# Moving only the later half of the queries in the recurrence heads of a hybrid decoder layer

## The chip, the cores and the metric

The kernel runs on one core of a Trainium2 chip. The metric is the time of one execution in device microseconds. Engines are named as in the profile: PE (TensorE; PEld is its loading of stationary operands), DVE (VectorE), ACT (ScalarE), POOL (GpSimd) and SP, whose queue issues most transfers.

## The reference

One layer over 1040 tokens (16 meta tokens and 1024 real ones), model width 1024:

```
h = h + 1/2 * SwiGLU_1(RMSNorm(h))
u = RMSNorm(h) @ W_in
o = concat[ HGRN2(u_hgrn) , StickBreaking(u_sb) ]
h = h + o @ W_out
h = h + 1/2 * SwiGLU_2(RMSNorm(h))
```

The change lies in HGRN2, a gated linear recurrence with four heads of key and value width 128, worked in chunks of 128 tokens:

```
bcum = cumsum(log f);  decay[t,s] = exp(bcum[t] - bcum[s]) for s <= t
attn[t,s] = sum_d q[t,d] k[s,d] decay[t,s,d];   o = (q exp(bcum)) S + attn v
S_new = exp(b_last) S + (k exp(b_last - bcum))^T v
```

followed by a normalisation of each head's output and a gate. The decay differs for each key column d, so the attention inside a chunk is no single matmul.

## The kernel before, in words

All projections and both feed-forward parts are matmuls in halves: an operand is split into a rounded high part (`wh`, `xh`, `oT`...) and a low part, and three products are summed. The recurrence works in plain float32, and each of its 128x128 matmuls shows in the trace as two passes (two LDWEIGHTS, two MATMUL).

`hgrn_attend(h, ...)` is a generator that does one recurrence head. It builds the attention of all eight chunks by levels n = 1, 2, 4, 8, 16, 32, 64. At level n a chunk is cut into blocks of 2n tokens, and the later n tokens of each block attend to the earlier n. The tiles hold the factors up to the block borders: QA is the query side, KB the key side (head dimension on partitions, tokens along the row), and F and `Ts` hold products of forget factors. A level has three parts.

- Scores (`scores`, L855): for each chunk KB is the stationary operand and QA the moving one, all 128 queries of it. Four chunks fill one PSUM bank, tile `lvl` of pool `pz`; a level fills two such banks, and the pool has two.
- Only the part where later queries meet earlier keys is kept in `attn`: by a predicated copy on DVE up to n = 8 (L886), by block copies on ACT from n = 16 on (L877).
- Then DVE multiplies QA and KB by their factors (L904, L908) and makes the next `Ts` (L914). These overwrite what the scores read, and the next level's scores need them.

After the levels the head transposes KB (`km` for the meta tokens, `knp`, L920 and L927), copies them to SBUF, makes the state of the first chunk from the meta tokens (`s`, L934, copied by DVE at L935) and the updates (`up`, L941), and runs the state through the chunks on DVE (L944). Two halves of the output follow (`op`, L954 and L957), with squares and roots on ACT, a multiplication on DVE (L967), transposes (`onp`, L973), gain and gate (L975) and a split into oH (L980, L981). At its start it transposes the values (`flip`, tile vT) and copies the meta part `vm` on DVE (L845).

PSUM here has four pools of two banks: `pz` (tag z), `ptr` (tag tr), `po` (tag o) and `pproj2`, for the product that runs beside the heads. With a tag's two banks in turn, a tile waits until the last reader of the tile two before it is done.

The heads are woven by `weave` with the first half of the product o @ W_out: 64 steps of three `wo` matmuls (L1267) on the attention heads' output oT. Below, heads 0 to 3 are A to D; A, B and C run beside each other, and D follows A. `weave` writes the order of PE by hand: each `yield a, b` of a head states the PE time a that the step took and the delay b until its next step is due, and two totals (the last arguments) set how the product's steps are spread over the heads' work. So the yielded numbers fix PE's order, which is kept as written. The order on DVE, ACT, POOL and SP is made by a scheduler from estimates. Each engine works its own order strictly in turn.

## Time and profile before

| | |
|---|---|
| median of 3 runs (lowest to highest) | 2064.65 us (2059.46 to 2064.86) |
| the profiled execution | 2062.77 us |
| its span, first to last instruction | 2061.0 us |
| granted TensorE clock | 1.000 |
| busy: PE, DVE, ACT, POOL | 2004.8, 1376.6, 901.2, 638.6 us |
| MATMUL passes of `lvl` (L855) | 512, from 1215.6 to 1340.7 us |

Times inside the execution are microseconds from the start of the span. The four heads with the first half of the product last from about 1213 us to 1369 us; before that come the first feed-forward part, the projections and the attention heads, after it the second half of the product and the second feed-forward part. A busy PE in the page is an upper figure: a matmul's row lasts longer than the step from one matmul to the next, since they are pipelined. What PE really needs is read from the starts of consecutive rows.

### The profile page before, as it was taken

What the parts mean: (1) busy time and instruction counts of PE and PEld (TensorE: products, weight loads), DVE (VectorE), ACT (ScalarE), POOL (GpSimd) and SP (SyncE); (2) the same over time, 40 slices, a digit from 0 to 9 for tenths busy, and PEclk for the clock granted to TensorE, in tenths of its full rate; (3) what the DMA queues carried; (4) which work ended last, traced back from release to release, by engine and by line L of the source; (5) the groups of instructions that cost most, each with busy time, mean ns of one, the idle gap of its engine ahead of it and who ended that gap; (6) DMA issues with size and microseconds to landing.
All of it is one profiled execution on the core that took longest, in us unless ns stands there. A gap on an engine that the chain in (4) does not pass through costs nothing.

```text
span 2061.0 us, 31571 instructions
## 1 busy us (share of the span) xinstructions
PE 2004.8 (97%) x11249; PEld 1782.3 (86%) x11249; DVE 1376.6 (67%) x2069; ACT 901.2 (44%) x1855; POOL 638.6 (31%) x696
## 2 busy tenths in 40 slices
PE   7999999999999999999999999999999999999999
PEld 7999999999987899988887878888888888878887
DVE  6867745556688842257878757648677677666774
ACT  7633332334554534456666623336333333234443
POOL 2366644542000002243443300210564454441000
PEclk9999999999999999999999999999999999999999
DMA  8643322227875645435454262684343333349573
GB/s 237 192 145 113 112 79 94 99 76 232 285 219 171 226 135 169 147 123 130 116 144 114 64 223 88 195 272 137 112 131 105 95 110 102 97 150 346 185 229 113
DMA packets 289647, 314.96 MB, mean 153 GB/s; under 512 B 24080, under 2 KB 218000, under 8 KB 289488
## 3 DMA queue, kind: packets, MB, share of 16 engines
q1 hardware_dynamic: 272304, 260.83, 41.1%
q0 software_dynamic: 16144, 52.10, 6.6%
q8 instruction: 89, 1.46, 0.3%
q14 instruction: 70, 0.57, 0.1%
q10 hardware_dynamic: 1040, 0.00, 0.0%
HBM read 228.62 MB, written 84.23 MB: 152 GB/s over the span
## 4 chain that ended last, share of the span: by engine, by line
PE 83%; DVE 7%; DMA 3%; ACT 3%; issue 2%; POOL 0%; SPq 0%; DVEq 0%; POOLq 0%; ACTq 0%
PE o L599 16%; PE qb L313 15%; PE qa L313 10%; PE qc L313 10%; PE proj L162 5%; PE proj L160 5%; PE proj L161 5%; PE qd L313 4%; PE o L561 3%; PE wo L1267 3%; PE flip L1086 2%; DVE wl L270 1%; PE lvl L855 1%; DVE keep L1232 1%; PE oacc L1156 1%
## 5 line engine op out<-in xcount | busy, mean ns | idle before, releaser
L313 PE MATMUL qb<-T,wh 128*128 128x384 f32 (+1 forms) x1056 | 317.8, 362 | 0.0
L270 DVE TENSOR_TENSOR wl<-s,wh 128x512 fp32r<-128x512 f32 x176 | 198.8, 1130 | 95.2 <-ACT wh L268 91.1
L313 PEld LDWEIGHTS qb<-T,wh 128*128 128x128 f32 x1056 | 195.8, 188 | 21.5
L313 PE MATMUL qa<-B,wh 128*128 128x384 f32 (+1 forms) x704 | 213.9, 367 | 0.3 <-ACT sg L415 0.3
L599 PE MATMUL o<-wl,th 128*128 128x512 f32 x539 | 209.9, 391 | 3.7 <-DVE wl L520 3.7
L599 PE MATMUL o<-wh,tl 128*128 128x512 f32 x539 | 209.6, 390 | 0.7 <-DVE tl L520 0.7
L599 PE MATMUL o<-wh,th 128*128 128x512 f32 x539 | 209.9, 391 | 0.0
L268 ACT CAST wh<-s 128x512 fp32r<-128x512 f32 x176 | 109.4, 621 | 223.2 <-PE qb L313 164.1
L160 PE MATMUL proj<-xh,wh 128*128 128x384 f32 (+2 forms) x576 | 205.0, 356 | 0.2 <-ACT xh L250 0.2
L270 DVE TENSOR_TENSOR wl<-raw,wh 128x512 fp32r<-128x512 f32 x184 | 170.1, 926 | 52.2 <-ACT wh L268 48.7
L161 PE MATMUL proj<-xh,wl 128*128 128x384 f32 (+2 forms) x576 | 199.1, 346 | 0.0
L162 PE MATMUL proj<-xl,wh 128*128 128x384 f32 (+2 forms) x576 | 198.9, 345 | 0.1
L268 ACT CAST wh<-raw 128x512 fp32r<-128x512 f32 x184 | 113.6, 620 | 184.1 <-PE qc L313 100.4
L313 PE MATMUL qb<-T,wl 128*128 128x384 f32 (+1 forms) x528 | 192.0, 364 | 0.9 <-DVE wl L270 0.9
L518 ACT CAST th<-act 128x512 fp32r<-128x512 f32 (+2 forms) x176 | 96.6, 550 | 178.1 <-PE o L599 120.0
L520 DVE TENSOR_TENSOR tl<-act,th 128x512 fp32r<-128x512 f32 (+2 forms) x176 | 105.5, 602 | 64.9 <-ACT th L518 63.7
L313 PE MATMUL qd<-X,wh 128*128 128x272 f32 x704 | 144.4, 292 | 2.0 <-DVE sp L397 1.6
L283 POOL TENSOR_TENSOR s<-raw 128x512 f32<-128x512 f32 x88 | 122.6, 1393 | 74.8 <-DVE wl L270 60.1
L313 PEld LDWEIGHTS qa<-B,wh 128*128 128x128 f32 x704 | 130.5, 188 | 16.5 <-ACT sg L415 0.7
L1232 DVE TENSOR_TENSOR_SCAN keep<-keep 128x144 f32<-128x144 f32 (+6 forms) x112 | 127.1, 1138 | 8.3 <-ACT keep L1228 6.0
L1237 POOL TENSOR_TENSOR sig<-sig,keep 128x144 f32<-128x144 f32 (+3 forms) x64 | 88.2, 1378 | 141.7 <-DVE keep L1232 75.6
L313 PE MATMUL qa<-B,wl 128*128 128x384 f32 (+1 forms) x352 | 128.8, 366 | 0.8 <-DVE wl L270 0.8
(343 smaller groups left out, 4761.1 us busy)
## 6 DMA issues: line engine op xcount, KB each, us to landing
raw<-in_ffn_w_in_dram SPq DMA_DIRECT2D x228, 256.0 KB, 3.0
raw<-in_ffn_w_out_dram SPq DMA_DIRECT2D x176, 256.0 KB, 4.3
raw<-in_w_in_dram SPq DMA_DIRECT2D x28, 512.0 KB, 4.5
ks<-kD SPq DMA_DIRECT2D x32, 260.0 KB, 5.6
oT<-oD SPq DMA_DIRECT2D x32, 256.0 KB, 4.7
ak<-in_ffn_w_out_dram SPq DMA_DIRECT2D x22, 256.0 KB, 5.3
v<-vD SPq DMA_DIRECT2D x8, 576.0 KB, 4.8
vD<-vhl SPq DMA_DIRECT2D x8, 512.0 KB, 3.9
```

What stands on the lines that cost most here:

```text
L160: nc.tensor.matmul(ps, wh[:, s], xs, start=k == 0, stop=False)
L161: nc.tensor.matmul(ps, wl[:, s], xs, start=False, stop=False)
L162: nc.tensor.matmul(ps, wh[:, s], xl[:, k, c0 : c0 + n], start=False, stop=k == nk - 1)
L268: nc.scalar.copy(hi, src)
L270: nc.vector.tensor_sub(lo, src, hi.bitcast(F32))
L283: op(t, x, y)
L313: nc.tensor.matmul(ps, a[:, k, :], b[:, k0 + k, :], start=start and k == 0 and i == 0, stop=k == 3 and i == 2, skip_group_check=True,)
L518: nc.scalar.copy(hi, src)
L520: nc.vector.tensor_sub(lo, src, hi.bitcast(F32))
L599: nc.tensor.matmul(banks[bank][m], z[:, m * P : (m + 1) * P], y, start=start and q == 0 and e == 0, stop=q == nq - 1 and e == 2, skip_grou ...
L1232: nc.vector.tensor_tensor_scan(out=kv, data0=kv, data1=kv, initial=1.0 if last else keep[:, end : end + 1], op0=ALU.mult, op1=ALU.bypass,)
L1237: nc.gpsimd.tensor_mul(sig, sig, keep[:, 1 : nk + 1])
```

## The change

It has five edits, all in `hgrn_attend` and the call of `weave`.

1. From n = 4 on, the scores move only the later-half queries of each block: a matmul has 64 moving columns where it had 128, and the eight chunks of a level fill one bank where they filled two. The stationary operand and the number of matmuls stay. The copies become one of 512 elements per partition in place of two of 256 (n = 4, 8), and half as many on ACT, twice as wide.
2. A level's factors on QA and KB are written ahead of its copies into `attn`.
3. The small tiles `vmp`, `km` and `s` go from the tr banks to the o banks.
4. The copies of `vm` and of the first state go from DVE to ACT.
5. Levels from n = 4 yield 960 in place of 1740, and the total work handed to `weave` is 4 * 18000 in place of 4 * 21900.

```diff
-        ps = self.flip(vT, [(0, META)])
-        nc.vector.tensor_copy(vm, ps[:META, 0, :])
+        ps = self.po.tile([P, P], F32, tag="o", name="vmp")
+        nc.tensor.transpose(ps[:META, :], vT[:, :META], self.ident)
+        nc.scalar.copy(vm, ps[:META, :])
...
         def later(x, n):
 
+            if len(x.shape) == 3:
+                return x.rearrange("p c (b h r) -> p c b h r", h=2, r=n)[:, :, :, 1, :]
             return x.rearrange("p (b h r) -> p b h r", h=2, r=n)[:, :, 1, :]
 
         def level(i, n):
+
             nb = P // (2 * n)
-            m = later(self.masks[:, i, :], n).unsqueeze(1).broadcast_to([P, 4, nb, n])
-            for half in range(2):
-                ps = scores(half)
-                if n >= 16:
-                    for s in range(0, P, 2 * n):
-                        nc.scalar.copy(
-                            attn[half][s : s + n, :, s + n : s + 2 * n],
-                            ps[s : s + n, :, s + n : s + 2 * n],
-                        )
-                    continue
-                out, src = (
-                    x.rearrange("p c (b h r) -> p c b h r", h=2, r=n)[:, :, :, 1, :]
-                    for x in (attn[half], ps)
+            m = later(self.masks[:, i, :], n)
+            if n < 4:
+                m = m.unsqueeze(1).broadcast_to([P, 4, nb, n])
+                return [
+                    (later(attn[half], n), m, later(scores(half), n)) for half in range(2)
+                ]
+            ps = self.pz.tile([P, 8, P // 2], F32, tag="z", name="lvl")
+            for c in range(8):
+                nc.tensor.matmul(
+                    ps[:, c, :].rearrange("p (b r) -> p b r", r=n),
+                    KB[:, META + c * P : META + (c + 1) * P],
+                    later(QA[:, c * P : (c + 1) * P], n), start=True, stop=True,
                 )
-                nc.vector.copy_predicated(out, m, src)
+            if n < 16:
+                m = m.unsqueeze(1).broadcast_to([P, 8, nb, n])
+                return [(later(at8, n), m, ps.rearrange("p c (b r) -> p c b r", r=n))]
+            return [
+                (at8[s : s + n, :, s + n : s + 2 * n], None, ps[s : s + n, :, s // 2 : s // 2 + n])
+                for s in range(0, P, 2 * n)
+            ]
...
         for i, n in enumerate(LEVELS):
-            level(i, n)
+            copies = level(i, n)
...
                 kb[:, :, 0, :], kb[:, :, 0, :], tk[:, :, 1:2].broadcast_to([P, nb, n])
             )
+            for out, m, got in copies:
+                if m is None:
+                    nc.scalar.copy(out, got)
+                else:
+                    nc.vector.copy_predicated(out, m, got)
...
-            yield 1740, 2600
+            yield 960 if n >= 4 else 1740, 2600
         dec = tn
 
-        km = self.ptr.tile([P, P], F32, tag="tr", name="km")
+        km = self.po.tile([P, P], F32, tag="o", name="km")
...
-        ps = self.ptr.tile([P, P], F32, tag="tr", name="s0")
+        ps = self.po.tile([P, P], F32, tag="o", name="s0")
         nc.tensor.matmul(ps, kms, vm, start=True, stop=True)
-        nc.vector.tensor_copy(S[:, 0, :], ps)
+        nc.scalar.copy(S[:, 0, :], ps)
...
-                        self.weave(first_half_of_o(), lanes, 64 * 680.0 + 5000.0, 4 * 21900.0)
+                        self.weave(first_half_of_o(), lanes, 64 * 680.0 + 5000.0, 4 * 18000.0)
```

The edits also move instructions. On PE, in the levels of heads A, B and C, before (one row per run of like matmuls; `lvl` are scores, `wo` the product beside):

```order
L1086 MATMUL flip<-ident,vT 128x128 x8
L855 MATMUL lvl<-QA,KB 128x128 x168
L920 MATMUL km<-ident,KB 16x128
L927 MATMUL knp<-ident,KB 128x128 x8
L920 MATMUL km<-ident,KB 16x128
L927 MATMUL knp<-ident,KB 128x128 x8
```

The same stretch now, up to the second group of `wo`:

```order
L1100 MATMUL flip<-ident,vT 128x128 x8
L856 MATMUL lvl<-QA,KB 128x128 x48
L884 MATMUL lvl<-QA,KB 128x64 x16
L1281 MATMUL wo<-wh,oT 128x512
L1281 MATMUL wo<-wl,oT 128x512
L1281 MATMUL wo<-wh,oT 128x512
L856 MATMUL lvl<-QA,KB 128x128 x8
L884 MATMUL lvl<-QA,KB 128x64 x16
L1281 MATMUL wo<-wh,oT 128x512
L1281 MATMUL wo<-wl,oT 128x512
L1281 MATMUL wo<-wh,oT 128x512
L884 MATMUL lvl<-QA,KB 128x64 x24
```

Three more such groups of three follow, so that 15 `wo` matmuls stand ahead of the first `km` where none did. From there on the count of `wo` that stand ahead of each step is 15 higher than before, up to the last `op` of head D.

On DVE, at level n = 2 of heads A and B, before (`wl` is the low part of a W_out tile, split for `wo`; the L886 rows are the copies into `attn`):

```order
L886 COPY_PREDICATED attn<-masks,lvl 128x128x2 x2
L904 TENSOR_TENSOR QA<-QA,Ts 128x256x2
L908 TENSOR_TENSOR KB<-KB,Ts 128x260x2
L886 COPY_PREDICATED attn<-masks,lvl 128x128x2
L914 TENSOR_TENSOR Ts<-F 128x520
L886 COPY_PREDICATED attn<-masks,lvl 128x128x2
L904 TENSOR_TENSOR QA<-QA,Ts 128x256x2
L908 TENSOR_TENSOR KB<-KB,Ts 128x260x2
```

And now:

```order
L913 TENSOR_TENSOR QA<-QA,Ts 128x256x2
L917 TENSOR_TENSOR KB<-KB,Ts 128x260x2
L924 COPY_PREDICATED attn<-masks,lvl 128x128x2 x2
L147 TENSOR_TENSOR wl<-raw,wh 128x512 x2
L924 COPY_PREDICATED attn<-masks,lvl 128x128x2
L928 TENSOR_TENSOR Ts<-Ts 128x130
L913 TENSOR_TENSOR QA<-QA,Ts 128x256x2
L917 TENSOR_TENSOR KB<-KB,Ts 128x260x2
L924 COPY_PREDICATED attn<-masks,lvl 128x128x2
```

The factors stand ahead of the copies, and two splits stand inside level n = 2: of these the first stood behind level n = 8 of A and B, the second behind the first factors of n = 16. The third to fifth splits now stand ahead of A's and B's level n = 8.

On PE, at the end of head D, before (the last `op` of its second half, then the product, then the transposes of its output, then the product again, ending on oH, the heads' own output):

```order
L957 MATMUL op<-vr,attn 128x128
L1267 MATMUL wo<-wh,oT 128x512
L1267 MATMUL wo<-wl,oT 128x512
L1267 MATMUL wo<-wh,oT 128x512 x2
L1267 MATMUL wo<-wl,oT 128x512
L1267 MATMUL wo<-wh,oT 128x512 x2
L1267 MATMUL wo<-wl,oT 128x512
L1267 MATMUL wo<-wh,oT 128x512 x2
L1267 MATMUL wo<-wl,oT 128x512
L1267 MATMUL wo<-wh,oT 128x512 x2
L1267 MATMUL wo<-wl,oT 128x512
L1267 MATMUL wo<-wh,oT 128x512
```

Then come the eight `onp` rows and nine more `wo` on oT. Now:

```order
L971 MATMUL op<-vr,attn 128x128
L1281 MATMUL wo<-wh,oT 128x512
L1281 MATMUL wo<-wl,oT 128x512
L1281 MATMUL wo<-wh,oT 128x512 x2
L1281 MATMUL wo<-wl,oT 128x512
L1281 MATMUL wo<-wh,oT 128x512 x2
L1281 MATMUL wo<-wl,oT 128x512
L1281 MATMUL wo<-wh,oT 128x512
L987 MATMUL onp<-ident,vT 128x128 x8
L1281 MATMUL wo<-wh,oH_13950 128x512
```

Nine `wo` stand between the last `op` and `onp` in place of 15, and none on oT stand behind `onp`.

On SP's queue the load of the second normalisation's gain (`g2r`) now stands ahead of the first six loads of the second feed-forward part's weights; it stood behind them. On ACT, seven high parts of W_out tiles now stand ahead of the first copy of a level n = 16; two did.

## The prediction

> **What bounds the kernel now.** I read the page first: its busy shares and, in the chain that ended last, the shares by engine.

> ```profile
> PE 2004.8 (97%) x11249; PEld 1782.3 (86%) x11249; DVE 1376.6 (67%) x2069; ACT 901.2 (44%) x1855; POOL 638.6 (31%) x696
> PE 83%; DVE 7%; DMA 3%; ACT 3%; issue 2%; POOL 0%; SPq 0%; DVEq 0%; POOLq 0%; ACTq 0%
> ```

> PE bounds the kernel as a whole, so a change gains where it takes work from PE or lets it idle less. The heads are one stretch of it. The second view is the table by windows over that stretch: start and end, length, then busy time (instructions) of PE, PEld, DVE, ACT and POOL, granted clock, DMA share, GB/s.

> ```profile
> 1215.00:1245.00 30.00, 26.61 (x212) 24.20 (x211) 28.07 (x50) 3.48 (x6) 0.00 (x0) 1.00 0.53 178
> 1245.00:1265.00 20.00, 19.33 (x163) 18.35 (x162) 18.39 (x41) 9.98 (x39) 0.00 (x0) 1.00 0.17 53
> 1265.00:1283.00 18.00, 14.33 (x101) 11.94 (x100) 11.36 (x28) 7.07 (x16) 0.00 (x0) 1.00 0.39 122
> 1305.00:1340.00 35.00, 34.05 (x213) 29.98 (x213) 23.41 (x38) 8.37 (x28) 5.73 (x8) 1.00 0.65 199
> ```

> DVE is nearly always busy while heads A, B and C make their small levels; later PE is nearly full. The real need of PE follows from starts: sixteen score matmuls of head D took 1.79 us as pieces of the chain (0.112 each pass), six of the product 1.40 (0.233 each).

> ```profile
> 1304.99 1.79 PE lvl L855 x16
> 1306.78 1.40 PE wo L1267 x6
> ```

> In the first two windows no product runs: 212 x 0.112 = 23.7 of 30 us and 163 x 0.112 = 18.3 of 20 us. PE idles 6.3 and 1.7 there, 8.0 together. The third view, groups by line and tile over the stretch, says for whom `lvl` waited at the PE itself (4.3 us) and what the copies cost.

> ```profile
> L855 PE MATMUL lvl<-QA,KB 128*128 128x128 f32 x512 | 63.7, 279 | 4.3 <-DVE attn L886 2.5 <-ACT attn L877 1.3 <-DVE attn L864 0.2
> L886 DVE COPY_PREDICATED attn<-masks,lvl 128x256 f32<-128x256 uint8 x32 | 17.7, 577 | 4.4 <-PE lvl L855 4.0
> ```

> **Edit 1, narrow scores.** 4 heads x 5 levels x 8 matmuls x 2 passes = 320 passes move 64 columns in place of 128. No score of before does that. The nearest row is a matmul that moves a single column through a 128x128 stationary operand (L173, elsewhere in the kernel), seen in three short windows of the timeline, each of which begins one pass later:

> ```profile
> 569.99 0.47 PE L173 MATMUL nps<-ones_d,nacc 128*128 128x1 f32 x3
> 570.10 0.47 PE L173 MATMUL nps<-ones_d,nacc 128*128 128x1 f32 x3
> 570.21 0.38 PE L173 MATMUL nps<-ones_d,nacc 128*128 128x1 f32 x3
> ```

> These start 0.11 us apart with one column moved, as against 0.112 with 128. So the pass is set by something that the edit leaves alone, and that comes once per matmul; the load of the stationary operand is the candidate. I take 0: between 1 and 128 columns lie 0.002 us, at most 0.6 us for all 320 passes. The other bound is a pass half as long, 0.056, 17.9 us of PE work; what that would give is a rival below.

> [...]

> The copies on DVE up to n = 8 become one of 512 elements. From DVE's timeline, where x2 means two in a row:

> ```profile
> 1248.19 0.77 DVE L886 COPY_PREDICATED attn<-masks,lvl 128x256 f32<-128x256 uint8 x2
> 1248.87 0.68 DVE L904 TENSOR_TENSOR QA<-QA,Ts 128x512 f32<-128x512 f32 x1
> 1249.47 0.69 DVE L908 TENSOR_TENSOR KB<-KB,Ts 128x520 f32<-128x520 f32 x1
> 1250.38 0.68 DVE L147 TENSOR_TENSOR wl<-raw,wh 128x512 fp32r<-128x512 f32 x1
> ```

> Two copies take 0.68 us from start to next start, one multiplication of 512 elements 0.60. One copy of 512 lies between 0.60 and 0.68: at most 0.08 x 6 = 0.5 us on the busy DVE of A to C.

> **Edits 2 and 5, with one bank per level: the order.** By the new order 15 `wo` stand ahead of the first `km`, one group of three per round of levels from n = 4 on, and five splits (`wl`, 0.61 us each on DVE) move up into n = 2 to n = 8. There DVE is the full engine (28.07 of 30 us), so its part grows by 5 x 0.61 = 3.1, less some of the 0.5 of the copies: +2.7. The two groups of `wo` there (2 x 3 x 0.233 = 1.4) fit into PE's 6.3 idle. Three groups, 2.1 us, fall in the rounds from n = 16, where three heads need 48 x 0.112 = 5.4 us of PE a round against 3 x (0.60 + 0.61) = 3.6 of DVE: there PE pays. Factors ahead of copies, and a level that needs one bank, take away part of the 4.3 us that `lvl` waited, and the splits leave that part of DVE: I give them 0.8. So the levels of A to C end 2.7 + 2.1 - 0.8 = 4.0 later, and everything behind has 15 x 0.233 = 3.5 us less to do: **+0.5**. Bounds: nothing longer (-3.5) and 3.1 + 2.1 longer (+1.7).

> **Edits 3 and 4: small tiles and copies.** The waits view for PE, on the stretch (total, times, longest):

> ```profile
> PE knp L927 <- ACT vT L928: 1.2, 2, 0.7
> PE flip L1086 <- DVE vm L845: 1.1, 1, 1.1
> PE op L954 <- ACT sq L962: 0.8, 1, 0.8
> PE lvl L855 <- ACT attn L877: 0.9, 1, 0.9
> PE km L920 <- DVE F L944: 0.9, 1, 0.9
> PE s L934 <- DVE F L944: 0.7, 1, 0.7
> PE up L941 <- DVE F L935: 0.4, 1, 0.4
> PE knp L927 <- DVE kms L921: 0.4, 1, 0.4
> ```

> Between the levels and head C's transposes `km` and `s` waited for tr banks that DVE's state steps (L944) had to leave; the o banks are free then for A and B, and the state copy leaves DVE. Of 1.2 + 0.9 + 0.7 + 0.4 + 0.4 = 3.6 us, those for `km`, `s`, `up` and `kms` (2.4) should go, with a little of the first: **-2.6**, between -1.2 (only `km` and `s` less what `knp` then waits) and -3.6.

> Against it, `s` of head C stands amid the outputs of A and B. Its o bank is the one that L967 of the first of these must leave. Timelines of PE and DVE:

> ```profile
> 1287.03 0.48 PE L934 MATMUL s<-vm,kms 16*128 16x128 f32 x2
> 1287.44 1.83 PE L941 MATMUL up<-vr,vT 128*128 128x128 f32 x14
> 1289.29 0.68 DVE L967 TENSOR_TENSOR vT<-op,ss 128x512 f32<-128x512 f32 x1
> 1290.12 0.46 PE L954 MATMUL op<-F,QA 128*128 128x128 f32 x2 [0.84 <-ACT sq L962]
> ```

> `s` ran at 1287.03, and the third `op` already waited for a bank, until 1290.12. Now `s` cannot start before 1289.29 + 0.68 = 1289.97; with `s` and `up` (0.41 + 1.7) behind it the third `op` comes at about 1292.1: **+2.0**. Bounds: 0, if the order of bank release leaves another one free, and 1289.97 - 1287.03 = 2.9. Queued behind `s` are `up`, the outputs and, by DVE's state steps, head C.

> The wait of `flip` for `vm` goes, since `vmp` no longer takes a tr bank (**-1.1**; 0 if the copy on ACT is as late). Of the waits of `lvl` for ACT one of 0.9 stands in head D; with one bank per level it goes (**-0.9**; 0 to -0.9).

> **The end of head D.** Nine `wo` (2.1 us) in place of 15 (3.5) now cover the work between the last `op` and `onp`. Before:

> ```profile
> 1363.28 0.69 DVE L967 TENSOR_TENSOR vT<-op,ss 128x512 f32<-128x512 f32 x1
> 1365.71 1.04 PE L973 MATMUL onp<-ident,vT 128*128 128x128 f32 x8
> 1365.91 0.62 ACT L145 CAST wh<-raw 128x512 fp32r<-128x512 f32 x1 [2.88 <-PE wo L1267]
> 1366.35 1.41 DVE L975 SCALAR_TENSOR_TENSOR attn<-onp,og,KB 128x512 f32<-128x512 f32 x2 [1.74 <-PE onp L973]
> ```

> `vT` was done at 1363.97, about 3.0 us after the last `op`, so 2.1 us of cover leave 0.9. ACT now has casts (0.62) between the squares, and half 0's gain (L975, 1.41 / 2) may stand ahead of half 1's multiplication. I take 0.9 + 0.7: **+1.6**, between 0 and 0.9 + 0.62 x 2 + 0.7 + 0.9 = 3.7, the last 0.9 for `onp` itself with nothing beside it.

> **Outside the heads.** The gain `g2r` is now loaded ahead of six weight tiles. Before:

> ```profile
> 1381.15 1.29 DVE L238 SCALAR_TENSOR_TENSOR xn<-hm,rs,g2r 128x1024 f32<-128x1024 f32 x1 [1.69 <-DMA g2r<-in_ffn_norm_dram]
> 1383.09 0.50 PE L1267 MATMUL wo<-wh,oH 128*128 128x512 f32 x1 [0.63 <-DVE hm L1693]
> ```

> DVE stood 1.69 for it, and PE behind DVE 0.63: **-0.8** (0 to -1.1). Two `vm` copies on ACT at the heads' start delay `vr`: **+0.3** (0 to 0.6).

> Sum: 0 + 0.5 - 2.6 + 2.0 - 1.1 - 0.9 + 1.6 - 0.8 + 0.3 = -1.0. The profiled execution took 2062.77 us, so 2061.8; it lies 1.9 below the median of the runs shown, by which it would be 2063.6. I say 2062.5. The low bounds add up to -0.6 - 3.5 - 3.6 - 1.1 - 0.9 - 1.1 = -10.8, the high ones to 1.7 - 1.2 + 2.9 + 3.7 + 0.6 = +7.7; half of each, since they will not fall together, gives the forecast's own range of 2057 to 2067.

> **Rivals.** (1) The narrow pass costs half. Then 80 passes of head D save 80 x 0.056 = 4.5 us where PE is full; of the 240 of A to C, where DVE keeps pace, at most PE's share from n = 16, 144 x 0.056 = 8.1, less what DVE limits, some 6. 2061.8 - 10.5 = 2051. For: half the columns. Against: the one-column rows. By this rival edit 1 does what its words promise, and by the forecast it does not.

> (2) All 15 `wo` fall into PE's 8.0 us of idle ahead of `km`, the levels end no later: 2061.8 - 4.0 = 2057.8. For: 8.0 exceeds 3.5. Against: DVE's 28.07 of 30, to which the splits come.

> (3) Slower: the splits in the full DVE part wait for their weights. The third split needs the third raw tile, whose buffer comes free with the first split; in between lie a load and a cast (0.62), against about 4.7 us of DVE work standing between the two splits. Rows of the loads (median us from issue to landing) and of the chain of waits:

> ```profile
> raw<-in_w_out_dram SPq DMA_DIRECT2D x10, 256.0 KB, 2.8
> 1204.69 8.75 DMA QA<-hg_q
> ```

> At 2.8 it fits. A load as long as the heads' own, 8.75, gives a stall of 8.75 + 0.62 - 4.7 = 4.7 on DVE with the factors of three heads queued behind it, and delayed casts on ACT hold the copies from n = 16 for another 1: 2061.8 + 5.7 = 2067.5, slower than before. It decides from a landing of about 4 us. For: seven casts stand ahead of the first copy of n = 16. Against: few other loads run then.

> **How the numbers follow.** Forecast 0.60, rivals 0.11, 0.17 and 0.12. A measurement here tells about 0.3%, 6.2 us, from no change. Faster than 2058.4 are the first rival, half of the second and 0.06 of the forecast: 0.25. Slower than 2070.9 are a third of the third and 0.05: 0.09. The range goes from 2053 to 2069: the first rival and the ends of the third lie outside.

> **What would show it.** Starts of 64-column passes 0.11 apart (0.056 would make rival 1 right); `wl` rows without a DMA ahead of them between 1225 and 1250; the first `km` about 4 us later; `s` of C waiting for L967; idle PE ahead of D's `onp`; no wait for `g2r`. A first `km` not later at all means that I took DVE for too full, and wrong waits in the outputs that the bank terms fail.

## The result: slower by 0.8%, at a lower TensorE clock

| | median (lowest to highest), us | runs | ratio to before, 95% interval |
|---|---|---|---|
| before | 2064.09 (2059.46 to 2066.57) | 7 | |
| changed | 2082.33 (2067.65 to 2085.47) | 7 | 1.008 (1.0064 to 1.0096) |

I forecast no measurable change, 2062.5 us within 2053 to 2069. The measured time lies 13 us above the range. The profiled execution of the changed kernel took 2079.49 us, its span is 2077.7 us, and its mean granted TensorE clock is 0.990 where it was 1.000.

The page of the changed kernel: busy shares, the granted clock in 40 slices of 51.9 us, and the chain of waits by engine.

```profile
PE 2019.2 (97%) x11249; PEld 1799.4 (87%) x11249; DVE 1374.3 (66%) x2053; ACT 898.1 (43%) x1835; POOL 639.1 (31%) x696
PEclk9999999999999999999999997999999999999999
PE 87%; DVE 7%; ACT 2%; issue 2%; DMA 1%; POOL 0%; SPq 0%; DVEq 0%; POOLq 0%; ACTq 0%
```

PE is busy for 14 us more with the same 11249 matmuls, and one slice of the clock, from 1246.6 us, reads 7 tenths. The table by windows of the changed kernel (columns as before: PE, PEld, DVE, ACT, POOL, granted clock, DMA share, GB/s) shows where. Before, the clock was 1.00 in every such row.

```profile
1213.00:1245.00 32.00, 26.17 (x187) 24.36 (x187) 29.76 (x55) 4.42 (x8) 0.00 (x0) 0.89 0.54 179
1245.00:1265.00 20.00, 17.59 (x113) 16.73 (x112) 12.93 (x23) 4.01 (x12) 0.00 (x0) 0.77 0.11 34
1265.00:1290.00 25.00, 24.82 (x120) 23.78 (x120) 9.38 (x16) 6.55 (x15) 0.57 (x1) 0.57 0.22 66
1290.00:1370.00 80.00, 75.47 (x486) 66.39 (x486) 51.46 (x96) 24.45 (x84) 14.47 (x17) 0.98 0.62 196
```

From 1265 to 1290 us PE is busy nearly all the time, and does 120 matmuls in 25 us; DVE and ACT wait. Pieces of the chain of waits say what a narrow pass costs there:

```profile
1249.40 3.53 PE lvl L884 x32
1257.50 6.73 PE lvl L884 x32
1270.11 10.13 PE lvl L884 x48
1284.93 0.21 PE km L934
```

32 passes take 3.53 us at full clock, 0.110 each, and 6.73 us, 0.210 each, a few microseconds later. In windows of 4 us the clock reads 0.50 from 1257 to 1285 without a break.

First and last starts of scores and `km` place the loss (before, then changed; L856 are the wide scores, n = 1 and 2 and the diagonal):

```profile
L855 PE MATMUL lvl<-QA,KB x512: 270/275/377, 1215.6 to 1340.7; 128*128 128x128 f32 x171
L920 PE MATMUL km<-ident,KB x3: 272/272/277, 1266.4 to 1279.5; 128*16 128x128 f32 x3
```

```profile
L856 PE MATMUL lvl<-QA,KB x192: 271/275/423, 1211.9 to 1335.9; 128*128 128x128 f32 x192
L934 PE MATMUL km<-ident,KB x3: 273/273/421, 1284.7 to 1295.7; 128*16 128x128 f32 x3
```

From the first score to the first `km` it takes 1284.7 - 1211.9 = 72.8 us in place of 50.8. The same reading of the kernels below, from starts in their profiled executions (the stages follow each other; "km C" is the last `km` of heads A to C; the first score comes at 1211.9 us in one execution and at 1218.3 us in another, so these stages compare better than the ends of spans; e11_best_wo, e12_wo3, e13_wo6 and e15_best2 are told in the text only):

| kernel | first score to first km | to km C | to first op | to last op of D | to the end | median time, us | ratio to before, 95% interval | median clock |
|---|---|---|---|---|---|---|---|---|
| before | 50.8 | 13.1 | 3.9 | 77.5 | 700.2 | | | |
| changed | 72.8 | 11.0 | 4.8 | 80.5 | 696.7 | 2082.33 | 1.008 (1.0064 to 1.0096) | 0.990 |
| e1_wide | 62.7 | 10.2 | 4.8 | 79.0 | 696.4 | 2070.66 | 1.004 (1.0026 to 1.0055) | 0.9965 |
| e2_narrow | 63.3 | 17.3 | 4.3 | 76.3 | 701.0 | 2077.81 | 1.0076 (1.0058 to 1.0094) | 0.990 |
| e3_order | 58.4 | 13.3 | 5.4 | 80.5 | 696.5 | 2067.82 | 1.0024 (1.0013 to 1.0035) | 0.997 |
| e4_keys | 61.3 | 9.7 | 4.8 | 77.2 | 696.7 | 2064.06 | 1.0017 (1.0003 to 1.0031) | 0.996 |
| e5_trim | 48.3 | 14.2 | 6.0 | 76.4 | 700.9 | 2062.63 | 0.9995 (0.9986 to 1.0004) | 0.997 |
| e6_first | 61.2 | 12.9 | 3.9 | 77.7 | 699.8 | 2072.83 | 1.0047 (1.0029 to 1.0066) | 0.9985 |
| e7_banks | 50.7 | 10.2 | 4.8 | 80.4 | 700.0 | 2062.80 | 0.9996 (0.9987 to 1.0005) | 0.998 |
| e8_trim_km | 48.1 | 13.7 | 7.5 | 74.2 | 699.6 | 2060.36 | 0.9984 (0.9973 to 0.9994) | 0.997 |
| e9_copies | 72.1 | 12.1 | 7.8 | 78.6 | 699.7 | 2085.49 | 1.0113 (1.0092 to 1.0133) | 0.9865 |
| e10_best | 48.1 | 12.6 | 7.7 | 74.2 | 700.5 | 2060.14 | 0.9977 (0.9964 to 0.9989) | 0.997 |
| e14_moving | 50.4 | 15.0 | 6.3 | 77.1 | 699.9 | 2067.25 | 1.0014 (1.0005 to 1.0023) | 0.997 |

In the rows from e1_wide on the ratio is to runs of before on the same chip, whose medians lie between 2062.9 and 2065.3.

The waits for which PE idled in the changed kernel (total, times, longest):

```profile
PE lvl L856 <- DVE attn L924: 5.2, 6, 2.1
PE s L948 <- ACT sq L976: 2.5, 1, 2.5
PE onp L987 <- DVE vT L981: 2.0, 1, 2.0
PE lvl L884 <- ACT attn L922: 2.0, 2, 1.1
PE lvl L884 <- DVE attn L924: 1.1, 2, 0.6
PE knp L941 <- ACT vT L942: 0.7, 1, 0.7
```

They explain few of the 22 us. Two theories stood against each other at this point. **M**: the clock follows the share of time in which PE moves columns, and a narrow pass, which lasts as long as a wide one (0.110 us at full clock against 0.112), halves it. **S**: the clock falls because of stalls, which the new order on DVE makes longer in n = 1 and 2.

### The profile page after: what moved, and what is told of

Same layout as the page of the kernel before. It is cut to its first block, busy times and chain, and to the rows that moved or that the text cites. A ratio compares the mean times of both kernels' runs of the same rounds, so it can differ in the third digit from the quotient of the medians.

```text
span 2077.7 us, 31530 instructions
## 1 busy us (share of the span) xinstructions
PE 2019.2 (97%) x11249; PEld 1799.4 (87%) x11249; DVE 1374.3 (66%) x2053; ACT 898.1 (43%) x1835; POOL 639.1 (31%) x696
## 4 chain that ended last, share of the span: by engine, by line
PE 87%; DVE 7%; ACT 2%; issue 2%; DMA 1%; POOL 0%; SPq 0%; DVEq 0%; POOLq 0%; ACTq 0%
PE o L599 17%; PE qb L313 15%; PE qa L313 10%; PE qc L313 10%; PE proj L160 5%; PE proj L162 5%; PE proj L161 5%; PE wo L1281 4%; PE qd L313 4%; PE o L561 3%; PE lvl L884 2%; PE flip L1100 2%; DVE wl L270 2%; DVE keep L1246 1%; PE lvl L856 1%
## 6 DMA issues: line engine op xcount, KB each, us to landing
raw<-in_ffn_w_in_dram SPq DMA_DIRECT2D x228, 256.0 KB, 3.1
raw<-in_ffn_w_out_dram SPq DMA_DIRECT2D x176, 256.0 KB, 4.2
oT<-oD SPq DMA_DIRECT2D x32, 256.0 KB, 4.3
ak<-in_ffn_w_out_dram SPq DMA_DIRECT2D x22, 256.0 KB, 5.1
```

## Experiments: what lowers the clock

**e1_wide, wide scores put back.**

```diff
-            ps = self.pz.tile([P, 8, P // 2], F32, tag="z", name="lvl")
-            for c in range(8):
-                nc.tensor.matmul(... later(QA[:, c * P : (c + 1) * P], n) ...)
+            got = [scores(half) for half in range(2)]
```

> The changed kernel, but the scores from n = 4 on again move all 128 queries of a chunk into two banks per level; factors first, the small tiles' banks, the copies on ACT, and the order of PE stay as changed. Theory M (the TensorE clock falls where PE moves too few columns for its time, and narrow passes, 0.112 us apart at full clock with half the columns, do that): granted clock 1.00 from 1240 us on, the mean at 0.998 or more, first km near 1270 instead of 1284.7, time 2057 to 2064. Theory S (the clock falls because PE stalls 1 to 2.4 us at a time in levels n = 1 and 2, where five weight splits came forward on DVE): the stalls are still there, the clock is 0.50 for some 30 us again, time 2075 to 2085.

The table by windows of e1_wide and its waits:

```profile
1237.00:1253.00 16.00, 11.25 (x86) 10.31 (x86) 14.34 (x30) 2.48 (x4) 0.00 (x0) 1.00 0.30 92
1253.00:1285.00 32.00, 29.35 (x229) 26.79 (x229) 19.75 (x39) 12.84 (x48) 0.57 (x1) 1.00 0.22 71
```

```profile
PE lvl L856 <- DVE attn L918: 11.2, 12, 2.1
```

The clock is 1.00 through the levels with the stalls there, longer in sum than as changed (11.2 us against 5.2): as the only cause of the fall S fails, and M holds for the clock. But M's time does not: 2070.66 in place of at most 2064, and the first `km` 62.7 us after the first score. Something besides the clock lengthens the levels by 12 us.

**e2_narrow, narrow scores alone.** The kernel before with edit 1 only (score and copies of the changed kernel, copies where they were).

> The kernel before with only the narrow scores and their one bank and merged copies from n = 4 on; order of PE, place of the copies, the tr banks and the engines of the small copies as before. Theory M: the clock falls to 0.50 in the rounds from n = 4 of heads A to C, the mean is 0.985 to 0.995, time 2070 to 2090. Theory S: no splits come forward, the clock stays 1.00, time 2058 to 2066.

```profile
1237.00:1253.00 16.00, 14.93 (x105) 14.79 (x104) 13.82 (x26) 0.99 (x4) 0.00 (x0) 0.79 0.00 1
1253.00:1285.00 32.00, 29.74 (x147) 28.75 (x148) 13.97 (x30) 7.19 (x21) 0.00 (x0) 0.54 0.05 17
```

The same 32 us have 147 matmuls at 0.54, in place of 214 before:

```profile
1253.00:1285.00 32.00, 27.93 (x214) 25.07 (x215) 22.93 (x51) 14.46 (x42) 0.44 (x1) 1.00 0.35 111
```

The narrow scores alone make the kernel 0.76% slower. In the trace the clock falls some 2.8 us after the first narrow passes of n = 4, comes back after sixteen wide passes of head C's n = 2 (3.5 us at half clock), and falls again when all heads are at narrow levels.

**e9_copies, the changed kernel without edit 2.** The loop over `copies` stands ahead of the factors.

> The changed kernel with the copies of a level ahead of its factors again; narrow scores, banks, copies on ACT and PE's order as changed. If the late copies lengthen the levels here as they did alone (10.4 us there, without any fall of the clock): waits of lvl at n = 1 and 2 for the copies fall from 5.2 us to about 2.5 and the time falls by 2 to 8 us under the changed kernel's 2082. The clock goes to 0.50 for some 30 us all the same, since the passes stay narrow: time still 2072 or more. If the clock fell because of those stalls and not of the narrow passes, it stays at 1.00 and the time is 2066 or less.

The waits of `lvl` at n = 1 and 2 fell to 2.0 us, more than expected, but the kernel became no faster (1.0113). Its windows and the wait that took their place:

```profile
1253.00:1285.00 32.00, 31.18 (x139) 30.12 (x140) 10.60 (x18) 4.70 (x15) 0.57 (x1) 0.51 0.10 33
```

```profile
PE wo L1281 <- DVE wl L147: 2.5, 1, 2.5
```

The gain ran into the first moved `wo`, which now waits for its split, and then into the half clock, which sets the pace from there: the same 139 matmuls in these 32 us as in the changed kernel. The expected 2 to 8 us were wrong; that the clock falls without these stalls held. It did not fall without any wait: at 1252.90 us a narrow pass had waited 1.15 us for a copy on ACT, and the clock fell at 1253.45.

**e12_wo3 and e13_wo6, the same narrow passes with more product between them.** Only delays change, so that PE's order alternates eight narrow scores with three or six `wo`.

```diff
-            yield 960 if n >= 4 else 1740, 2600
+            yield 960 if n >= 4 else 1740, 3900 if n >= 4 else 2600 + ((0, 600, 1100, 0)[h] if n == 2 else 0)
```

> The changed kernel with other delays (3900 from n = 4 on, and 600 and 1100 more for heads B and C at n = 2), so that three product matmuls stand behind each head's eight narrow scores in place of behind three heads' 24. Share of time in which columns move, if a wide score pass moves for 0.107 of its 0.112 us and a product matmul for 0.213 of its 0.233: (16 x 0.053 + 3 x 0.213) / (16 x 0.112 + 3 x 0.233) = 0.60, against 0.52 as changed. Theory M (share): higher than as changed, so the clock is at 0.50 for a shorter time than 30 us, or not at all if the bound lies below 0.60. Theory N (any run of narrow passes): 0.50 as in the changed kernel.

> As e12_wo3 with six product matmuls behind each head's eight narrow scores (delays 6000, 1300 and 4000): share 0.66. Theory M: the clock stays at 1.00 in the levels or falls for no more than some 5 us, though the passes are as narrow as in the changed kernel, and the time is 2058 to 2070. Theory N: 0.50 while narrow passes run, some 20 us or more, and 2075 or more.

Windows of e12_wo3, then of e13_wo6:

```profile
1237.00:1253.00 16.00, 14.78 (x115) 13.80 (x115) 15.37 (x28) 2.48 (x4) 0.57 (x1) 1.00 0.35 109
1253.00:1285.00 32.00, 30.89 (x229) 27.66 (x229) 20.06 (x39) 9.09 (x26) 1.63 (x3) 1.00 0.48 149
```

```profile
1253.00:1285.00 32.00, 32.00 (x225) 29.40 (x224) 19.56 (x31) 5.97 (x19) 2.78 (x6) 1.00 0.60 187
```

In e12_wo3, with a share of 0.60 by its expectation's estimate, the clock stays at 1.00 through all levels, though every pass from n = 4 on is narrow: 229 matmuls in 32 us, where the changed kernel made 139. So narrow passes as such are not the cause; what differs is how much else moves in the same time (0.60 against 0.52, both estimates). e13_wo6 met its time (2067.41, in 2058 to 2070; ratio 1.0011, 1.0002 to 1.0020). e12_wo3 took 2074.99 (1.0054, 1.0034 to 1.0074): its new order makes the levels 62.4 us long and moves head C's steps late (`km` of C 18.8 us after the first), with stalls and short falls behind them, outside the question.

The figures of the share come from the runs: at half clock a product matmul takes 1.39 / 3 = 0.46 us as pieces of the changed kernel's chain, by consecutive starts 0.427, and a wide score pass in e2_narrow 0.213; half of these, 0.213 and 0.107, I take for the time of moving at full clock. For a narrow pass, which also takes 0.213 at half clock, I take half of a wide one, 0.053, since it has half the columns. That is an assumption, which the count further down bears out.

**e4_keys, fewer stationary columns, and e5_trim, fewer on both sides.**

```diff
+            nk = P - n if n >= 16 else P
...
-                    KB[:, META + c * P : META + (c + 1) * P],
+                    KB[:, META + c * P : META + c * P + nk],
```

> The changed kernel, but from n = 16 on the stationary operand of a score leaves out the last n keys, which no later query of that level needs (112, 96 and 64 columns for n = 16, 32, 64). If the stationary columns set the pass: 0.112 us apart at n = 16 down to 0.056 at n = 64 at full clock. Theory M: a shorter pass moves the same 64 columns in less time, so at n = 64 the share of time in which columns move is as high as with wide scores, the clock comes back to 1.00 in that round before km, and the time is 5 to 12 us under the changed kernel's 2082. Theory S: the clock falls as in the changed kernel and stays at 0.50 until km; only the shorter passes save, 2 to 5 us.

```diff
-                    ps[:, j, :], KB[:, META + c * P : META + (c + 1) * P],
-                    QA[:, c * P : (c + 1) * P], start=True, stop=True,
+                    ps[: P - n, j, n:], KB[:, META + c * P : META + (c + 1) * P - n],
+                    QA[:, c * P + n : (c + 1) * P], start=True, stop=True,
```

> The kernel before, but from n = 16 on a score leaves out the first n queries of a chunk and the last n keys, on both operands (112, 96 and 64 columns stationary and as many moving, at n = 16, 32, 64); two banks per level and everything else as before. Theory M (the clock follows the share of time in which columns move): both sides shrink together, so a pass is shorter (0.098, 0.084 and 0.056 us) and the share stays that of a wide pass; the clock stays at 1.00 in the levels. Saved: head D 16 x (0.014 + 0.028 + 0.056) = 1.6 us, heads A to C up to 4.7; time 1.5 to 6 us below before. Theory N (any score with fewer than 128 moving columns lets the clock fall): 0.50 in the last rounds before km, time 5 us or more above before.

Two neighbouring rows of e5_trim, whose starts give the length of sixteen 64-column passes:

```profile
1266.73 1.15 PE L855 MATMUL lvl<-QA,KB 128*64 128x64 f32 x16
1267.81 0.48 PE L934 MATMUL s<-vm,kms 16*128 16x128 f32 x2
```

Sixteen passes with 64 columns on both sides take 1.08 us, 0.058 each in most; with 64 moved and 128 stationary columns it was 0.110 each in the changed kernel. So the stationary side does set the pass here. In e4_keys the clock is at 0.50 only from about 1258 to 1272 us. It comes back 1.7 us ahead of round n = 64, behind passes of n = 32, whose stationary operand has 96 columns, and three `wo`. The median is 18 us under that of the changed kernel, where 5 to 12 were expected, but the twelve times fall into two groups, seven from 2060.64 to 2064.12 us and five from 2068.32 to 2072.14, and by the ratios the gain is some 13 us (1.0017 against 1.008). In e5_trim the clock stays at 1.00 in the levels, and they are 2.5 us shorter (48.3); theory N, that fewer than 128 columns suffice, fails. But the time is the same as before (0.9995): what the levels won is lost again between the first `km` and the first `op` (1.1 and 2.1 us longer), where the state steps on DVE are late, and where the clock now falls once (0.71 in 1277 to 1281) behind those stalls.

**e14_moving, fewer moving columns in full-length passes.** As e5_trim with all 128 keys stationary.

> The kernel before, where a score from n = 16 on leaves out the first n queries and keeps all 128 stationary keys: moved columns 112, 96 and 64 as in e5_trim, but the pass stays at 0.112 us. Theory M: share 0.83 and 0.71 at n = 16 and 32 (clock 1.00) and 0.48 at n = 64, so the clock falls to 0.50 only from the last round on, for 5 to 12 us, time 2 to 8 us above before. Theory N: it falls from n = 16 on, 15 us or more. If the share has nothing to do with it: as e5_trim, 1.00 in the levels.

```profile
1253.00:1268.50 15.50, 15.36 (x131) 14.67 (x130) 12.70 (x26) 9.56 (x38) 0.00 (x0) 1.00 0.10 35
1268.50:1277.00 8.50, 7.17 (x54) 6.16 (x54) 5.14 (x13) 4.11 (x9) 0.00 (x0) 1.00 0.54 184
1277.00:1289.00 12.00, 8.93 (x35) 7.40 (x34) 6.70 (x20) 3.02 (x5) 0.00 (x0) 0.59 0.39 124
```

The time came as expected (1.0014, +3 us), the place did not: the last narrow rounds of A and B, 32 passes or some 3.6 us, stayed at 1.00, and the fall came some 10 us later, behind stalls. So narrow passes with a share of 0.48 did not lower the clock here, where I had expected the change between 0.48 and 0.71; in the count that follows the falls end at 0.41.

**The share, counted in the traces.** The traces of this case record every change of the granted clock. From 1195 to 1420 us in the seventeen profiled executions, the changes within an execution lie whole multiples of 3.413 us apart: every stretch at 0.50 there lasts 1, 2, 3, 4, 9 or 10 such steps (in the changed kernel 1, 1, 9 and 1, from 1221.75, 1231.99, 1255.88 and 1307.08 us). For each step I counted, from the starts of matmuls, the share of time in which columns move (0.107 us for 128 columns of a score pass or transpose, 0.053 for 64, 0.213 for a product matmul, twice as much at half clock), and read the clock of the step behind it.

- At full clock, 32 steps were followed by half clock: 30 with a share of 0.06 to 0.38, and two with 0.41. Of the 984 that kept the clock none was below 0.386, and seven lie between that and 0.404.
- At half clock, all 39 steps with a share up to 0.738 were followed by another one, and all 32 from 0.745 on by full clock.

These are counts of this case, with the moving times taken above; what sets the clock is not shown by any run. In them the clock was lost behind every step below 0.386 and behind none above 0.41, and it came back behind every step from 0.745 on and behind none below. If a narrow pass is counted like a wide one, 0.107, the steps no longer separate: some with 0.76 lose the clock and others with 0.40 keep it.

This puts M and S together. Narrow passes without a wait have 0.053 / 0.112 = 0.48 at full clock, and with that it was kept: of the changed kernel's three stretches below, the first is one step of narrow passes, and the clock stays. The next step has a wait of 1.15 us for copies on ACT (at n = 16) among its narrow passes and a share of 0.28, and the clock falls. Then narrow passes move for 0.107 of 0.213 us, 0.50, which did not bring it back, though PE is busy for 29.89 of 30.72 us.

```profile
1249.06:1252.47 3.41, 3.41 (x32) 3.36 (x30) 2.84 (x6) 0.00 (x0) 0.00 (x0) 1.00 0.00 0
1252.47:1255.88 3.41, 2.26 (x21) 2.12 (x20) 1.80 (x3) 1.02 (x4) 0.00 (x0) 1.00 0.00 0
1255.88:1286.60 30.72, 29.89 (x132) 28.81 (x132) 12.53 (x21) 6.56 (x18) 0.57 (x1) 0.50 0.13 43
```

With wide passes (0.107 / 0.112 = 0.96) a step comes below 0.386 only by some 2.0 us of waiting, with narrow ones by some 0.7, estimates from these shares. Stalls alone did it too: in the changed kernel single steps at 0.50 began at 1221.7 and 1232.0 us, ahead of its first narrow pass (1236.5), behind steps of 0.31 and 0.32. And e1_wide, with stalls of up to 2.1 us, has no step below 0.45 in its levels.

No long gap of PE was needed: the clock fell behind a gap of 1.15 us among narrow passes (changed kernel and e9_copies), and behind one of 2.5 us in e7_banks. The changed kernel's row for the 32 us of the other tables:

```profile
1253.00:1285.00 32.00, 30.11 (x139) 29.06 (x140) 12.35 (x22) 6.28 (x20) 0.57 (x1) 0.55 0.13 41
```

## Experiments: what else lengthens the levels

**e3_order, PE's order alone.**

```diff
-            yield 1740, 2600
+            yield 960 if n >= 4 else 1740, 2600
-                        self.weave(first_half_of_o(), lanes, 64 * 680.0 + 5000.0, 4 * 21900.0)
+                        self.weave(first_half_of_o(), lanes, 64 * 680.0 + 5000.0, 4 * 18000.0)
```

> The kernel before with only the yields of 960 from n = 4 on and the total of 4 * 18000, so 15 product matmuls move ahead of the first km. Theory M: scores are wide, clock 1.00, time 2060 to 2067 (a forecast term of +0.5). Theory S: if the splits come forward on DVE as in the changed kernel, PE stalls and the clock falls for some 30 us, time 2072 or more.

```profile
PE lvl L855 <- DVE attn L886: 4.2, 5, 2.4
PE lvl L855 <- DVE KB L908: 2.6, 2, 2.4
PE wo L1267 <- DVE wl L147: 2.1, 1, 2.1
```

Wide scores and the order as changed: 4.9 us slower in the medians, between the two expectations. The first moved `wo` waits 2.1 us for its split on DVE, scores behind it wait for copies and factors that stand behind the splits, and the clock falls for a few microseconds (0.76 and 0.82 in 1249 to 1257) after these stalls. The levels last 7.6 us longer, the part behind the last `op` is 3.7 shorter.

**e6_first, factors ahead of copies alone.**

```diff
-            level(i, n)
+            got = [scores(half) for half in range(2)]
...
+            level(i, n, got)
             o = 0 if n <= 8 else 1
```

> The kernel before with only the factors of a level written ahead of its copies. Theory W (this edit lengthens the levels: a score bank is read only after 1.2 us of factors, so PE waits longer for banks): waits of lvl for the copies on DVE grow from 2.5 us to 5 us or more, first km 3 to 5 us later after the first score, time 2 to 6 us above before. My prediction's reading (the edit shortens waits of lvl): first km no later, time within 2 us of before.

```profile
PE lvl L855 <- DVE attn L886: 12.0, 10, 2.1
```

```profile
1237.00:1253.00 16.00, 10.25 (x81) 9.48 (x82) 14.58 (x32) 3.52 (x6) 0.00 (x0) 1.00 0.29 91
```

The wait of scores for the copies on DVE grew from 2.5 to 12.0 us, the levels from 50.8 to 61.2 us, at a clock of 1.00: 81 matmuls where before made 121 in the same window (row of before below). The time is 9 us longer, more than theory W's 2 to 6.

```profile
1237.00:1253.00 16.00, 15.13 (x121) 13.78 (x120) 15.44 (x36) 2.59 (x13) 0.00 (x0) 1.00 0.04 15
```

The reason is the turn of the two score banks in the program. A copy ends the use of a bank; with 1.2 us of factors ahead of it, the next head's scores get their bank 1.2 us later each time. At the small levels, where DVE is the full engine (14.58 of 16 us in the row above), PE then has nothing else to do.

**e7_banks, small tiles in the o banks and copies on ACT.** The edits 3 and 4 as in the change.

> The kernel before with only the small tiles in the o banks and the copies of vm and of the first state on ACT. By the prediction's terms: the waits of km, s and up on DVE's state steps go (-2.6), flip's wait for vm goes (-1.1), s of head C waits for an o bank (+2.0), vm on ACT +0.3: 1.4 us below before. Rival (the bank wait of s costs more than it frees, 2.5 us as in the changed kernel, and the clock falls behind such a stall): 0 to 4 us above before.

```profile
L921 PE MATMUL km<-ident,KB x3: 272/272/273, 1267.0 to 1277.2; 128*16 128x128 f32 x3
```

```profile
PE s L935 <- ACT sq L963: 2.5, 1, 2.5
```

From first to last `km` 10.2 us in place of 13.1, as the term of -2.6 had it; against that `s` of head C waits 2.5 us for the squares of an output (the term of +2.0), and the clock reads 0.57 in the 4 us behind it (1289 to 1293). Together: no difference (0.9996).

## A version that beats both

**e8_trim_km, e10_best, e11_best_wo and e15_best2** put together what had paid: scores trimmed on both sides, the small tiles in the o banks, but `s` in the tr banks for all heads (e8_trim_km) or for head C alone (the others).

> The trimmed scores of the kernel before, with the small tiles vmp and km in the o banks and the copies of vm and of the first state on ACT, but s left in the tr banks. If the terms add up: e5_trim's gain and another 1 to 3 us, with no wait of 2.5 us of s for the squares of an output. If s waits for DVE's state steps in the tr bank all the same, no more than e5_trim.

> Trimmed scores (both sides from n = 16), vmp, km and s in the o banks and the copies of vm and of the first state on ACT, except s of head C, which stays in the tr banks; order of PE as before. From the runs so far: levels 48.2 us up to the first km instead of 50.8, 10.2 us instead of 13.1 from there to head C's km, and no wait of 2.5 us of head C's s: 5 to 7 us below before in all. If s of head C waits in the tr bank for the second half of the updates as long as in the o bank: 2 to 3 us below before.

```diff
-        ps = self.ptr.tile([P, P], F32, tag="tr", name="s0")
+        where, tag = (self.ptr, "tr") if h == 2 else (self.po, "o")
+        ps = where.tile([P, P], F32, tag=tag, name="s0")
```

> As e10_best, with the delay after a head's km step at 3500 in place of 2000, so that one group of three product matmuls stands between the last scores of head C and s of head A, where PE waited for DVE's state steps. If PE idles there: another 0.7 us less than e10_best. If what follows on DVE is the bound: no difference.

> As e10_best, with a head's update step split in two (after four of its seven updates), so that groups of product matmuls stand in the stall of 2.6 us that up has for DVE's state steps. If PE's idle time there is filled and the clock's fall behind it goes: 2 to 4 us under e10_best. If the outputs come later by as much: no difference.

e8_trim_km is 0.16% faster than before, e10_best 0.23% (0.9977, 0.9964 to 0.9989), 5.2 us in the medians, where 5 to 7 were expected. The levels are 2.7 us shorter; `s` of C no longer waits. What is left is a wait for the state steps on DVE:

```profile
PE up L943 <- DVE F L946: 3.1, 2, 2.6
```

The clock fell behind it (0.50 in 1273 to 1277). Three `wo` ahead of that place (e11_best_wo, 0.9981, 0.9969 to 0.9992) changed nothing. Groups of them inside the updates (e15_best2, 0.9977, 0.9966 to 0.9987) took the stall and the fall away there, and the time is no better than that of e10_best, as its second expectation had it: from the first `km` to C's it takes 8.8 us in place of 12.6, but the stage up to the last `op` grew from 74.2 to 83.5 us.

## Why the prediction was wrong, step by step

- **Edit 1 at 0.** The price of a pass was right (0.110 us for 64 columns at full clock, 0.112 for 128). The step that failed stands behind it: "I take 0" held the clock at 1.00, as it was in every window of before. I looked at what a pass costs and not at what it leaves PE doing: with half the columns in a pass of the same length, a wait of 1.15 us took the clock to 0.50, and it stayed there for 30.7 us. Alone, edit 1 costs 0.76%, some 15 us (e2_narrow). In the changed kernel it makes the difference between 1.004 and 1.008 (e1_wide against the change). By the estimate above, wide passes would have left room for some 2.0 us of waiting.
- **The levels of A to C 4.0 longer.** Measured: 22.0, of which e1_wide shows 11.9 without a fall of the clock. The wrong term is "factors ahead of copies ... take away part of the 4.3 us": I gave it 0.8 of gain, and it costs 10.4 us alone. In e1_wide `lvl` waits 11.2 us for the copies on DVE, where it was 2.5 before; that is 8.7 of the 11.9. I had priced what DVE does and not how long a bank is held. My bound for the stage, at most 5.2 longer, failed with it. The order alone took 7.6 (at most 5.2 by my terms): splits and `wo` in the full DVE part also stall PE, which the sum of DVE work did not show. The two do not add up (10.4 + 7.6 against 11.9). I suppose that stalls of the one are filled by the `wo` of the other, which no run shows. In the changed kernel, copies first again (e9_copies) did not shorten the levels (72.1 us), since half clock and the wait for a split set the pace there.
- **3.5 us less to do behind.** Right: 700.2 to 696.7 us from the last `op` to the end, and 3.7 in e3_order.
- **-2.6 for km and s, +2.0 for s of C.** Right in mechanism and nearly in size (-2.9 from first to last `km` in e7_banks; a wait of 2.5). The bank that `s` needed was held by the squares on ACT, not by L967 as I had it.
- **flip, -1.1; lvl in head D, -0.9; g2r, -0.8.** The waits of `flip` for `vm` and of `wo` for `hm` are not among PE's waits of the changed kernel, and those of `lvl` for ACT stand in A to C now.
- **+1.6 before onp.** 2.0 measured, for the reason given (`vT` of half 1 late on DVE).
- **Rivals.** The first (a pass of half the length) and the third (splits that wait for their weights: DVE did not wait for them in the levels) did not come; nor did the second. The right one was missing: a kernel whose PE is as busy as before at half the clock.

## What to carry to other kernels

Ask of an edit that thins out PE's work not only what a pass costs but in what share of the time columns still move, and read the granted clock beside it: in these traces every step of 3.413 us with a share below 0.386 was followed by half clock. Narrow passes have 0.48 without a wait (an estimate), and one wait of 1.15 us among them was enough; with product matmuls between them, at an estimated 0.60, they kept the clock (e12_wo3). And once it was lost, 0.50 did not bring it back in the changed kernel's 30.7 us. Where fewer columns are wanted, try to take them off both operands: in e5_trim the pass shortened with them, from 0.112 to 0.058 us. And before putting other work ahead of the operation that frees a PSUM bank, count who waits for that bank: 1.2 us of factors ahead of a copy cost the kernel before 9 us, with 12.0 us of waits for the copies in place of 2.5 (e6_first).
